# Heads' value products, x's forms, pool gates and tail stores moved to other slots of a hand-ordered transformer block

## The chip, the cores and the metric

The kernel runs on one core of a Trainium2 chip. The metric is the device time of one execution in microseconds (us); the median of several executions is compared. Five engines work side by side, each through its own instructions in order: TensorE (PE, matrix products and 128x128 transposes; PEld is its loading of the stationary operand), VectorE (DVE), ScalarE (ACT), GpSimd (POOL) and SyncE (SP, which here only issues transfers). Products end up in PSUM, which the kernel uses as eight banks of 128 x 512 fp32.

## The reference

One layer of a block on x (256 tokens x 4096) with a memory of 256 tokens:

```
h = rmsnorm(x, g_mix_pre);  proj = h @ w_in            # 4096 -> q|k|v|gate_a (4 x 2048), u|gate_b (2 x 2048)
A: 16 heads of 128: chunk-causal attention over the own chunk of 64 and earlier ones, bias by relative distance
   y_a = attention * silu(gate_a)
B: 4 groups of 512: trailing mean of u over 2/4/8/16 tokens, minus u; a 512x512 map; a scale
   y_b = pooled * silu(gate_b)
x = x + rmsnorm(concat(y_a, y_b) @ w_out, g_mix_post)
m = rmsnorm(mem, g_mem);  q = rmsnorm(x, g_xa_pre) @ w_xq;  k, v = m @ w_xk, m @ w_xv
x = x + rmsnorm(cross_attention(q, k, v, 4 heads) @ w_xo, g_xa_post)
```

All data is fp32.

## The kernel before

**Precision.** An fp32 operand a is used as a = h + l, both in a rounded fp32 format: ACT copies (rounds) a to h, DVE computes l = a - h, and a product of two such operands takes three matmuls (h h, l h, h l: lines 308 to 310). Each weight piece of 128 x 1024 thus costs one ACT cast (L185, `wh`) and one DVE difference (L186, `wl`).

**Slots.** The weights are a stream of 648 pieces of 512 KB. `plan` writes the stream; piece i is multiplied in slot i (`mm`), 12 matmuls of 512 columns as a rule. The last loop of `block_kernel` goes through the slots and in each one issues, in this order: `firsts` (set by `first_at`), `jobs` (the casts and differences of a piece that PE needs two or three slots later, and the load of a later one), `tasks` (set by `at`), and then the slot's own matmuls. So a function's place in the lists is its place in every engine's instruction order. Five pieces of `wh` and `wl` fit into SBUF, four raw pieces.

**Pairs.** w_in and w_out are taken in pairs of strips, 32 slots a pair: A0, B0, A1, B1, A2, B2, A3, B3 (gate_a and v, then q and k, of four heads each), U0 to U3 (u and gate_b of a pool group), O0 to O3 (w_out). A pair goes over 16 chunks of two 128-row blocks of its input (two slots each). A0, B0 and O0 are direct: four products per slot. The others do chunks 4, 6, 8, 10, 12 and 14 with seven products instead of eight (a Strassen step: `quad_sums`, `quad_split`, `quad_rest` make sums of weights on DVE; 12 matmuls in the first slot, 9 in the second). A pair's products are collected in banks: four at its start, a fifth at slot 8, a sixth and a seventh at slot 9, until `early` (slot 30) and `late1`, `late2` at its end read them. Every other product takes a bank from a list, first in first out (`bank`), and gives it back when its reader is issued (`done`); whoever takes it next waits for that reader.

**Forms of x.** A0 uses x as loaded. For the pairs after it, `x_forms(c)` makes chunk c's normalised blocks: two scaled blocks (L535), then one difference (L543) or the four sums of `sums_of` (L385 to L388), then h and l of all of them (`split_copy`, L237 on ACT and L238 on DVE). The 16 chunks stand in slots 19 to 41, two in three slots, while A0 and B0 run; `load_x` is issued three slots ahead.

**Heads.** With e the end of a B pair, head j of its group has o = e + 6 + 7j: `head_scores` in slot o, `head_max` (L615, reads the scores' bank) first in o+1, `head_exp` o+2, `head_soft` o+3, `head_turn` (three transposes) o+5, `head_turned` first in o+6, `head_att` (value product, L600 and L651) in o+8, `head_y` (multiply with the gate, L659) o+9, `y_store` (to a scratch in DRAM) o+11. `a_keep` turns the two gate results into `sg` (two `turn`s: four transposes each into a bank, then an ACT copy, L488) and makes v's h and l.

**Pool.** After pair U g: `pool_u` turns u, `pool_sum` and `pool_d` make the means for two halves b on DVE (with an h on ACT and an l on DVE), `pool_gates` runs `gate` twice (tanh on ACT, L494, then DVE, L495; one buffer for the tanh), `pool_turn` turns the gates into `sg`, two slots of pool products follow at slots 8 and 9 of the next pair, and `pool_y` collects a result and multiplies (L319, L320, L731).

**Memory norm and tail.** `rm.all_at` puts the sums over squares of the memory (`Rms.sums`, L269), their root and its use into successive slots. The last eight output blocks are made tokens-first, half t of the tokens after the other: `tail_stat` squares a result from its bank with its sum (L1069), `tail_root` and `tail_spread` make the norm, `tail_copy` copies the bank (L1086), `tail_turn` transposes it, `tail_gain`, `tail_scale` (L1104) and `tail_out` (L1110, add and store) finish. A store is issued by the ACT queue if POOL added, and by SP if DVE did.

Of the kernel before, what the change touches and what calls it, by code (L numbers as in the profile page):

```python
# [12 lines left out]
AF = mybir.ActivationFunctionType  # L13
# [32 lines left out]
QUADS = KT // 2  # L46
# [63 lines left out]
def block_kernel(ctx: ExitStack, tc: tile.TileContext, x, mem, ws, relb, vecs, out):  # L110
    nc = tc.nc
# [25 lines left out]
    def buf(tag, shape, name, dtype=F32, bufs=1):  # L137
        return com.tile(shape, dtype, tag=tag, name=name, bufs=bufs)
# [3 lines left out]
    def at(i, f, *a):  # L142
        tasks.setdefault(i, []).append((f, a))

    def first_at(i, f, *a):

        firsts.setdefault(i, []).append((f, a))
# [4 lines left out]
    def tiles(ap):  # L152
        return ap.rearrange("p (a b) -> p a b", b=P)

    def tok(t):
        return slice(t * P, t * P + P)

    V, A, T_ = nc.vector, nc.scalar, nc.tensor
# [3 lines left out]
    ev = {k: buf(f"e_{k}", [P, 512], f"e_{k}") for k in ("t", "u2", "u3", "c")}  # L162
# [56 lines left out]
    for s in range(n):  # L219
# [6 lines left out]
        else:  # L226
            i = s - (2 if wide and m[1] > FAST[0] else 3)
# [7 lines left out]
    def split_copy(h, l, src):  # L235

        A.copy(h, src)  # L237
        V.tensor_sub(l, src, h.bitcast(F32))  # L238
# [84 lines left out]
    accs = {}  # L323
# [14 lines left out]
    def end(*key):  # L338
        return max(where[key].values())
# [4 lines left out]
    for tag, cs in (("Fb1", (0, 1, 2, 3)), ("Fb2", (5, 7)), ("Fa1", (4, 6, 8, 9, 11)), ("Fa2", (10, 12, 13, 14, 15))):  # L344
        o = 0
# [3 lines left out]
    for tag, cs in (("Fb1", (0, 1, 2, 3, 5, 7)), ("Fa1", (4, 6, 8, 9, 11)), ("Fa2", (10, 12, 13, 14, 15))):  # L349
        o = 0  # L350
# [13 lines left out]
    def block(stage, c):  # L364

        tag, o, u = HOME[stage, c]
        f = forms[tag][:, 256 * o:256 * (o + u)]
        return tiles(f[:, :u * P]), tiles(f[:, u * P:])
# [14 lines left out]
    def sums_of(a11, a21, a12, a22, dst):  # L383

        V.tensor_add(dst[:, 1, :], a21, a22)  # L385
        V.tensor_sub(dst[:, 2, :], dst[:, 1, :], a11)
        V.tensor_sub(dst[:, 3, :], a11, a21)
        V.tensor_sub(dst[:, 0, :], a12, dst[:, 2, :])  # L388
# [50 lines left out]
    def result(pair):  # L439

        names = ("t", "u3", "u2", "c") if pair[0] == "O" else ("t", "c", "u2", "u3")
        return dict(zip(("c11", "c21", "c12", "c22"), (ev[k] for k in names)))
# [48 lines left out]
    def gate(pair, k):  # L491

        g, th = result(pair)[k], hd["x7"][:, 512:]
        A.activation(th, g, AF.Tanh, scale=0.5)  # L494
        V.scalar_tensor_tensor(g, th, 1.0, g, op0=OP.add, op1=OP.mult)  # L495

    for pair in PAIRS:
        if pair not in DIRECT:
            at(slot[pair, FAST[-1], 1] + 1, early, pair)
        e = end_slot[pair]  # L500
# [5 lines left out]
    hd = {"x7": buf("X7", [P, 1024], "x7"), "x6": buf("X6", [P, 1024], "x6")}  # L506
# [20 lines left out]
    def x_forms(c):  # L527
        src = xch.pop((1, c))
        ft = tiles(hd["ft"][c % 2])
        R = tiles(rx.R)  # L530
        spots = ((6, 8), (0, 2)) if c in FAST else ((0, 2), (3, 5))
        for j in range(2):
            k = 2 * c + j
            a, b = spots[j]
            V.scalar_tensor_tensor(ft[:, a:b, :], tiles(src[:, j, :]), gv[:, G_MIX_PRE + k:G_MIX_PRE + k + 1], R,  # L535
                                   op0=OP.mult, op1=OP.mult)
        h, l = block("in", c)
        u = h.shape[1]
        if c in FAST:
            sums_of(ft[:, 6, :], ft[:, 7, :], ft[:, 0, :], ft[:, 1, :], ft[:, 2:6, :])  # L540
        else:
            q = ft[:, :6, :].rearrange("p (k f) b -> p k f b", f=3)
            V.tensor_sub(q[:, :, 2, :], q[:, :, 0, :], q[:, :, 1, :])  # L543
        split_copy(h, l, ft[:, :u, :])
        if c in FAST:
            j = FAST.index(c)
            e = hd["extra"][j // 4][:, 256 * (j % 4):256 * (j % 4) + 256]
            extra[c] = e[:, :P], e[:, P:]
            split_copy(*extra[c], ft[:, 7, :])
# [5 lines left out]
    first = KT // 2 + 3  # L555
    at(first - 3, x_buffers)
    for c in range(QUADS):
        i = first + (3 * c) // 2
        at(i - 3, load_x, c, 1)
        at(i, x_forms, c)  # L560


    def a_gates(hg):
# [101 lines left out]
    for hg in range(4):  # L665
        e = end_slot["A", hg]
        at(e + (3 if hg else 14), a_gates, hg)
        at(e + (9 if hg else 16), a_keep, hg)
        e = end_slot["B", hg]
        at(e + 2, b_turn, hg, 0)  # L670
        at(e + 3, b_turn, hg, 1)
        for j in range(4):
            h, o = 4 * hg + j, e + 6 + 7 * j
            at(o - 3, head_bias, h)
            at(o - 2, head_qk_split, h)
            at(o, head_scores, h)
            first_at(o + 1, head_max, h)
            at(o + 2, head_exp, h)
            at(o + 3, head_soft, h)
            at(o + 5, head_turn, h)  # L680
            first_at(o + 6, head_turned, h)
            at(o + 8, head_att, h)
            at(o + 9, head_y, h)
            at(o + 11, y_store, h, "sg", j)


    pg = {}
# [27 lines left out]
        hl = pg["d"][b]  # L715
        split_copy(hl[:, :, :S], hl[:, :, S:], d)

    def pool_gates(g):
        gate(("U", g), "c12")
        gate(("U", g), "c22")  # L720

    def pool_turn(g):
        for t, k in enumerate(("c12", "c22")):
            turn(("U", g), k, hd["sg"][:, :, tok(t)], 0.5)
# [8 lines left out]
    for g in range(4):  # L733
        e = end_slot["U", g]
        at(e + 2, pool_u, g)
        i = [e + 3, e + 4]
        for b in range(2):
            for j in range(g + 1):
                at(i[b], pool_sum, g, b, j)
            at(i[b] + 1, pool_d, g, b)  # L740
        at(e + 5, pool_gates, g)
        at(e + 7, pool_turn, g)
        for c in range(4):
            j = end("pool", g, c)
            at(j + 1 + c % 2, pool_y, g, c)
            at(j + 3 + c % 2, y_store, 16 + 4 * g + c, "sg", c)


# [18 lines left out]
    for c in range(QUADS):  # L767
        i = slot[("O", 0), c, 0] - 3
# [7 lines left out]
    def x2(k, m=1):  # L776
        return x2t[k // 4][:, k % 4:k % 4 + m, :]
# [12 lines left out]
    for m in range(4):  # L790
        e = end_slot["O", m]
# [29 lines left out]
    rm = Rms("m", None, None, None, None)  # L821
# [18 lines left out]
    def m_pass(slots, home, stat=False):  # L840

        for kt, i, j in slots:
            if kt % 2 == 0:
                at(j, load_m, kt // 2, home)
            at(i, m_prep, kt, stat)
            if stat and kt % 2:
                at(i + 1, rm.add)

    uses = sorted(where["xk",].items())
    at(uses[0][1] - 8, late_buffers)  # L850
    m_pass([(k, i - 3, i - 6) for k, i in uses], 0, True)
    rm.all_at(uses[-1][1] - 1)
    m_pass([(k, i - 2, i - 6) for k, i in sorted(where["xv", 1].items())], 1)

    kv = {}
# [56 lines left out]
    b = e_out + 10  # L912
    room = begin("xq", 0) - b - 1
    for c in range(KT // 2):
        i = b + (c * room) // (KT // 2)
# [79 lines left out]
    e = end("xq", 7)  # L995
    for h in range(XH):
        i = end("xq", 2 * h + 1)
# [4 lines left out]
    for h in (0, 1):  # L1002
        i = end("xq", 2 * h + 1)
# [8 lines left out]
    e = end("xv", 1)  # L1012
# [23 lines left out]
    for c in range(first_tail):  # L1036
        e = end("xo", c) + 1
# [20 lines left out]
    zs = const.tile([P, 2, 2], F32, name="zs")  # L1058
# [6 lines left out]
        done(rz.p)  # L1065

    def tail_stat(t, j):
        a = accs["xo", j, t]
        A.activation(ev["u2"], a, AF.Square, accum_out=zs[:, t, j:j + 1])  # L1069
        b = z["b"] = z["base"][:, t:t + 1] if j == 0 else z["b"]  # L1070
        v = const.tile([P, 1], F32, name=f"v_z{t}{j}")
        V.tensor_scalar(v, zs[:, t, j:j + 1], 1.0 / D, b, op0=OP.mult, op1=OP.add)
        z["b"] = v
# [34 lines left out]
    def tail_out(t, eng, a, b):  # L1108
        y = y2["y"][:, a:b, tok(t)]
        eng.tensor_add(y, y, x2(a, b - a)[:, :, tok(t)])  # L1110
        (nc.scalar if eng is nc.gpsimd else nc.sync).dma_start(out[:, a:b, tok(t)], y)

    v, g = nc.vector, nc.gpsimd
    s_, o_ = tail_scale, tail_out
    at(n - TAIL + 3, tail_base)
    for t in range(2):
        e = n - TAIL // 2 + TAIL * t
        at(e, tail_stat, t, 0)
        at(e, tail_copy, t, 0)
        at(e + 1, tail_turn, t, 0)  # L1120
        at(e + 2, tail_gain, t, 0)
    e = n
    at(e, tail_stat, 0, 1)
    at(e, tail_root, 0)
    at(e, tail_copy, 0, 1)
    at(e + 2, tail_turn, 0, 1)
    at(e + 2, tail_spread, 0)
    at(e + 3, tail_gain, 0, 1)
# [1 line left out]
    for i, steps in enumerate((((s_, 0, 4), (o_, g, 0, 4), (s_, 4, 12), (o_, v, 4, 8)),  # L1130
# [3 lines left out]
        for f, *a in steps:  # L1134
            at(e + 3 + i, f, 0, *a)
    e = n + TAIL
    at(e, tail_stat, 1, 1)
    at(e, tail_root, 1)
    at(e, tail_copy, 1, 1)
    at(e, tail_turn, 1, 1)  # L1140
    at(e, tail_spread, 1)
    for f, *a in ((s_, 0, 4), (o_, v, 0, 4), (s_, 4, 12), (o_, g, 4, 8), (s_, 12, 16), (o_, g, 8, 12), (s_, 16, 24),
# [156 lines left out]
```

## Time and profile before

| | |
|---|---|
| median of 3 runs | 1888.58 us (1888.17 to 1889.97) |
| profiled execution | 1889.54 us, span 1887.8 us |
| PE, DVE, ACT busy | 97%, 79%, 55% of the span |
| mean granted TensorE clock | 0.987 of full speed |

The span runs from the first to the last instruction. Idle time stands in brackets, with what ended it. A matmul's duration overlaps the next one's, so PE's rate is read from start to start.

### The profile page before, as it was taken

To read this page: it belongs to the slowest core of one execution; us is meant where nothing else is said; L and a number is where in the kernel's file an instruction comes from. 1 tells how busy PE (TensorE), PEld (TensorE's weight loads), DVE (VectorE), ACT (ScalarE), POOL (GpSimd) and SP (SyncE) were. 2 spreads that over 40 slices of the span, in tenths; PEclk is the share of its full clock that TensorE was granted. 3 is DMA by queue.
4 is the path that set the end of the run, shared out by engine and by line. 5 is a ranking of instruction groups with operands and counts; after the bars stand their busy time and mean duration, and the time that the engine had idled before them with its cause. 6 is when DMAs were issued, how large, how long until landed. Compare 5 with 4: busy or idle time off the path is not lost.

```text
span 1887.8 us, 23776 instructions
## 1 busy us (share of the span) xinstructions
PE 1823.7 (97%) x8404; PEld 1508.0 (80%) x8404; DVE 1498.0 (79%) x1999; ACT 1033.6 (55%) x1411; POOL 17.3 (1%) x20
## 2 busy tenths in 40 slices
PE   9989999999999999999999999999999999999996
PEld 7867878877887788777888787888888888888885
DVE  8875687978797889787989898769788899656686
ACT  8455454645554555454545465555555677545552
POOL 0000000000000000000000000000000000000002
PEclk9999999999999999999999999999999999999998
DMA  8756555655565556454656476756565777556654
GB/s 291 235 189 214 168 184 178 212 189 178 184 221 167 181 195 219 168 178 156 217 173 226 168 242 206 257 170 213 186 215 182 240 259 256 189 173 215 208 186 121
DMA packets 122920, 378.14 MB, mean 200 GB/s; under 512 B 12976, under 2 KB 27440, under 8 KB 122800
## 3 DMA queue, kind: packets, MB, share of 16 engines
q1 hardware_dynamic: 118432, 374.25, 59.5%
q10 hardware_dynamic: 4368, 2.36, 0.4%
q8 instruction: 66, 1.08, 0.2%
q14 instruction: 54, 0.44, 0.1%
HBM read 368.17 MB, written 8.39 MB: 199 GB/s over the span
## 4 chain that ended last, share of the span: by engine, by line
PE 85%; DVE 8%; issue 3%; ACT 2%; DMA 1%; POOL 0%; SPq 0%; ACTq 0%; DVEq 0%; POOLq 0%
PE P L308 17%; PE P L309 17%; PE P L310 17%; PE acc L303 6%; DVE wl L186 3%; PE acc L304 3%; PE c L310 3%; PE c L308 3%; PE c L309 3%; ACT wh L185 1%; PE xk L308 1%; PE xv L309 1%; PE xk L309 1%; PE xv L310 1%; PE xv L308 1%
## 5 line engine op out<-in xcount | busy, mean ns | idle before, releaser
L186 DVE TENSOR_TENSOR wl<-raw,wh 128x1024 fp32r<-128x1024 f32 (+1 forms) x646 | 782.4, 1221 | 244.1 <-ACT wh L185 232.1
L185 ACT CAST wh<-raw 128x1024 fp32r<-128x1024 f32 (+1 forms) x646 | 672.0, 1049 | 349.0 <-PE P L309 78.9
L308 PE MATMUL P<-wh,Fa 128*128 128x512 f32 x938 | 370.9, 395 | 4.0 <-DVE x L320 3.8
L309 PE MATMUL P<-wh,Fa 128*128 128x512 f32 x938 | 367.8, 392 | 0.0
L310 PE MATMUL P<-wl,Fa 128*128 128x512 f32 x938 | 367.7, 392 | 0.0
L308 PE MATMUL P<-wh,Fb 128*128 128x512 f32 x588 | 234.2, 398 | 0.0
L310 PE MATMUL P<-wl,Fb 128*128 128x512 f32 x588 | 230.3, 392 | 0.0
L309 PE MATMUL P<-wh,Fb 128*128 128x512 f32 x588 | 230.3, 392 | 0.0
L185 ACT CAST wh<-tt 128x1024 fp32r<-128x1024 f32 (+1 forms) x156 | 123.8, 834 | 168.6 <-DVE tt L209 147.8
L308 PEld LDWEIGHTS P<-wh,Fa 128*128 128x128 f32 x938 | 178.2, 190 | 42.5 <-issue 4.9
L310 PEld LDWEIGHTS P<-wl,Fa 128*128 128x128 f32 x938 | 177.6, 189 | 37.6
L309 PEld LDWEIGHTS P<-wh,Fa 128*128 128x128 f32 x938 | 178.2, 190 | 35.8
L186 DVE TENSOR_TENSOR wl<-tt,wh 128x1024 fp32r<-128x1024 f32 (+1 forms) x156 | 143.4, 956 | 43.4 <-ACT wh L185 42.4
L310 PEld LDWEIGHTS P<-wl,Fb 128*128 128x128 f32 x588 | 111.2, 189 | 23.8
L309 PEld LDWEIGHTS P<-wh,Fb 128*128 128x128 f32 x588 | 111.6, 190 | 22.0
L308 PEld LDWEIGHTS P<-wh,Fb 128*128 128x128 f32 x588 | 111.5, 190 | 21.9
L310 PE MATMUL c<-wl,Fa 128*128 128x512 f32 x276 | 108.5, 393 | 3.1 <-DVE wl L186 3.1
L308 PE MATMUL c<-wh,Fa 128*128 128x512 f32 x276 | 108.5, 393 | 1.2 <-ACT wh L185 1.2
L309 PE MATMUL c<-wh,Fa 128*128 128x512 f32 x276 | 107.5, 390 | 0.0
L303 PE MATMUL acc<-h2HL,wh 128*128 128x512 f32 x256 | 91.4, 400 | 0.0
L304 PE MATMUL acc<-h2HL,wl 128*128 128x256 f32 x256 | 71.8, 281 | 0.0
L303 PE MATMUL acc<-xoHL,wh 128*128 128x512 f32 x192 | 66.9, 395 | 0.0
(291 smaller groups left out, 2405.0 us busy)
## 6 DMA issues: line engine op xcount, KB each, us to landing
raw<-ws_dram SPq DMA_DIRECT2D x647, 512.0 KB, 3.9
tt<-x_dram SPq DMA_DIRECT2D x31, 256.0 KB, 4.9
lc<-mem_dram SPq DMA_DIRECT2D x24, 256.0 KB, 4.4
yd<-sg SPq DMA_DIRECT2D x32, 128.0 KB, 4.6
yin<-yd SPq DMA_DIRECT2D x16, 256.0 KB, 5.0
lc<-x_dram SPq DMA_DIRECT2D x16, 256.0 KB, 4.3
x<-relb_dram SPq DMA_DIRECT2D x16, 192.0 KB, 4.5
e_u<-mem_dram SPq DMA_DIRECT2D x8, 256.0 KB, 4.1
```

The source lines that it names most:

```text
L185: A.copy(h[:, c], src[:, c])
L186: V.tensor_sub(l[:, c], src[:, c], h[:, c].bitcast(F32))
L303: T_.matmul(acc, H[:, w], X, start=first, stop=last, skip_group_check=True)
L304: T_.matmul(acc[:, :S], L[:, w], X[:, :S], start=False, stop=last, skip_group_check=True)
L308: T_.matmul(acc, xs[0], w[0], start=first, stop=False)
L309: T_.matmul(acc, xs[1], w[0], start=False, stop=False)
L310: T_.matmul(acc, xs[0], w[1], start=False, stop=last)
```

## The change

Five edits of order, none of arithmetic. (1) `x_forms` keeps the scaled blocks and sums and moves to the head of its slot (`first_at`); h and l move into `x_split`, at the head of the slot after. (2) `head_att`, `head_y` and `y_store` come one slot later, and `a_keep` of groups 1 to 3 too (slot 10 instead of 9). (3) The pool's two gates stand apart (slots e+4 and e+6 instead of both in e+5), group 0's sums and means come one slot later, `pool_turn` too (e+8); all four `pool_y` move to the head of the slot behind their product. (4) The memory's sums come one slot later. (5) In the tail the bank is copied before the square, which reads the copy; the stores of POOL's blocks of the first token half go out on SP's queue.

```
-        split_copy(h, l, ft[:, :u, :])
+    def x_split(c):
+        ft = tiles(hd["ft"][c % 2])
+        h, l = block("in", c)
+        split_copy(h, l, ft[:, :h.shape[1], :])
         if c in FAST:
...
-        at(i, x_forms, c)
+        first_at(i, x_forms, c)
+    for c in range(QUADS):
+        first_at(first + (3 * c) // 2 + 1, x_split, c)
...
-        at(e + (9 if hg else 16), a_keep, hg)
+        at(e + (10 if hg else 16), a_keep, hg)
...
-            at(o + 8, head_att, h)
-            at(o + 9, head_y, h)
-            at(o + 11, y_store, h, "sg", j)
+            at(o + 9, head_att, h)
+            at(o + 10, head_y, h)
+            at(o + 12, y_store, h, "sg", j)
...
         at(e + 2, pool_u, g)
-        i = [e + 3, e + 4]
         for b in range(2):
+            i = e + 3 + b + (g == 0)
             for j in range(g + 1):
-                at(i[b], pool_sum, g, b, j)
-            at(i[b] + 1, pool_d, g, b)
-        at(e + 5, pool_gates, g)
-        at(e + 7, pool_turn, g)
+                at(i, pool_sum, g, b, j)
+            at(i + 1, pool_d, g, b)
+            at(e + 4 + 2 * b, gate, ("U", g), ("c12", "c22")[b])
+        at(e + 8, pool_turn, g)
         for c in range(4):
             j = end("pool", g, c)
-            at(j + 1 + c % 2, pool_y, g, c)
+            first_at(j + 1, pool_y, g, c)
...
-    rm.all_at(uses[-1][1] - 1)
+    rm.all_at(uses[-1][1])
...
-        a = accs["xo", j, t]
-        A.activation(ev["u2"], a, AF.Square, accum_out=zs[:, t, j:j + 1])
+        A.activation(ev["u2"], ev["tc"[j]], AF.Square, accum_out=zs[:, t, j:j + 1])
...
-        (nc.scalar if eng is nc.gpsimd else nc.sync).dma_start(out[:, a:b, tok(t)], y)
+        (nc.scalar if t and eng is nc.gpsimd else nc.sync).dma_start(out[:, a:b, tok(t)], y)
...
-        at(e, tail_stat, t, 0)
         at(e, tail_copy, t, 0)
+        at(e + 1, tail_stat, t, 0)
...
+    at(e, tail_copy, 0, 1)
     at(e, tail_stat, 0, 1)
     at(e, tail_root, 0)
-    at(e, tail_copy, 0, 1)
...
+    at(e, tail_copy, 1, 1)
     at(e, tail_stat, 1, 1)
     at(e, tail_root, 1)
-    at(e, tail_copy, 1, 1)
```

## Rows read from the trace of the kernel before

**Rows 1.** The page, part 1: busy us (share of the span) xinstructions.

```profile
PE 1823.7 (97%) x8404; PEld 1508.0 (80%) x8404; DVE 1498.0 (79%) x1999; ACT 1033.6 (55%) x1411; POOL 17.3 (1%) x20
```

**Rows 2.** Timeline of PE, second head group: start, us, line, operation [idle before].

```profile
465.12 0.39 PE L308 MATMUL P<-wh,Fa 128*128 128x512 f32 x1
465.80 0.39 PE L308 MATMUL P<-wh,Fa 128*128 128x512 f32 x1
...
469.41 0.58 PE L600 MATMUL at<-ahl,vs 128*128 128x256 f32 x1 [2.77 <-DVE x L615]
```

**Rows 3.** Windows: us, busy of PE, PEld, DVE, ACT, POOL; PEclk; DMA share; GB/s.

```profile
80.00:90.00 10.00, 10.00 (x46) 8.29 (x45) 7.99 (x15) 4.09 (x6) 0.00 (x0) 1.00 0.59 185
101.00:147.00 46.00, 38.17 (x150) 26.61 (x150) 37.08 (x63) 23.63 (x32) 0.00 (x0) 1.00 0.53 175
284.50:292.00 7.50, 7.43 (x28) 6.21 (x29) 4.49 (x8) 3.44 (x7) 0.00 (x0) 0.77 0.42 134
838.50:846.50 8.00, 7.90 (x25) 6.52 (x26) 3.82 (x7) 2.73 (x5) 0.00 (x0) 0.61 0.40 125
```

**Rows 4.** Waits of PE: engine line waited for: us in total, times, longest.

```profile
PE at L600 <- DVE x L615: 23.3, 12, 2.8
PE tn L484 <- DVE e_u L495: 6.5, 5, 3.2
PE P L308 <- DVE x L320: 3.8, 2, 3.4
...
PE ms L269 <- DVE lc L261: 1.8, 1, 1.8
...
PE tn L1092 <- ACT e_t L1086: 0.6, 1, 0.6
```

**Rows 5.** Timeline of DVE, one cycle of x's forms in pair B0.

```profile
97.97 0.88 DVE L535 SCALAR_TENSOR_TENSOR ft<-tt,gv,x 128x256 f32<-128x256 f32 x2
...
100.21 0.96 DVE L238 TENSOR_TENSOR Fb<-ft,Fb 128x768 fp32r<-128x768 f32 x1 [0.90 <-ACT Fb L237]
101.16 2.36 DVE L186 TENSOR_TENSOR wl<-raw,wh 128x1024 fp32r<-128x1024 f32 x2
...
106.38 1.09 DVE L238 TENSOR_TENSOR Fa<-ft,Fa 128x896 fp32r<-128x896 f32 x1 [1.01 <-ACT Fa L237]
...
107.59 1.22 DVE L186 TENSOR_TENSOR wl<-raw,wh 128x1024 fp32r<-128x1024 f32 x1
108.72 0.88 DVE L535 SCALAR_TENSOR_TENSOR ft<-tt,gv,x 128x256 f32<-128x256 f32 x2
```

**Rows 6.** The page, part 6: the loads of x; last, us to landing.

```profile
tt<-x_dram SPq DMA_DIRECT2D x31, 256.0 KB, 4.9
```

**Rows 7.** Timeline of DVE in the second head group.

```profile
433.31 1.23 DVE L186 TENSOR_TENSOR wl<-raw,wh 128x1024 fp32r<-128x1024 f32 x1 [1.82 <-ACT wh L185]
...
468.81 0.55 DVE L615 SCALAR_TENSOR_TENSOR x<-sc,x 128x384 f32<-128x384 f32 x1
```

**Rows 8.** Timelines of PE and ACT at a_keep of the second group.

```profile
322.57 1.03 PE L484 MATMUL tn<-ident,e_u 128*128 128x128 f32 x8
...
325.20 2.00 ACT L185 CAST wh<-raw 128x1024 fp32r<-128x1024 f32 x2
```

**Rows 9.** Timelines of ACT, SP (group 0) and DVE (group 3), pool gates.

```profile
879.10 1.08 ACT L488 ACTIVATE sg<-tn 128x512 f32<-128x512 f32 x2 [5.63 <-DMA yd<-sg]
...
875.14 0.42 SPq L663 DMA_DIRECT2D yd<-sg  x1
...
1159.01 0.69 DVE L495 SCALAR_TENSOR_TENSOR e_u<-x,e_u 128x512 f32<-128x512 f32 x1 [0.70 <-ACT x L494]
```

**Rows 10.** Timelines of ACT, PE and DVE in the tail.

```profile
1870.80 0.60 ACT L1069 ACTIVATE e_u<-xo 128x512 f32<-128x512 f32 x1 [6.22 <-POOL y L1110]
...
1872.02 1.04 PE L1092 MATMUL tn<-ident,e_c 128*128 128x128 f32 x4 [2.62 <-ACT e_c L1086]
...
1873.58 0.69 DVE L1104 TENSOR_TENSOR y<-y,mr 128x512 f32<-128x512 f32 x1 [0.89 <-PE mr L1082]
```

More of the change, by code (lines that the diff above doesn't have):

```diff
@@ L536, in x_forms @@
                                    op0=OP.mult, op1=OP.mult)
-        h, l = block("in", c)
-        u = h.shape[1]
         if c in FAST:
@@ L716, in pool_d @@
         split_copy(hl[:, :, :S], hl[:, :, S:], d)
-    def pool_gates(g):
-        gate(("U", g), "c12")
-        gate(("U", g), "c22")
     def pool_turn(g):
```

## The prediction, made before the change was run

> **What bounds the kernel now.** I read the page's busy shares first [rows 1]: TensorE (PE) is at work 97% of the span, so the change can only win what PE loses: gaps, and stretches at the lower clock. At the full clock three of its 512-column matmuls start in 0.68 us, from 465.12 to 465.80 [rows 2], so 0.227 us each, and a slot of twelve takes 2.72 us. The windows [rows 3] show a full stretch (80 to 90), a stretch that loses (101 to 147) and two in which the granted clock is far below 1.00: after a long wait PE runs for some us at the lower of its levels, 1.2 GHz instead of 2.4. The share missing times the length is what that costs: 0.23 x 7.5 = 1.7 us in the first, which stands for six like it among the heads, 0.39 x 8.0 = 3.1 us in the second. PE's own waits [rows 4] then name the places: twelve waits of the heads' value products (L600), five before the pool's gate transposes, two for banks that the pool results free, one before the memory sums, one in the tail. The rest, but for the first loads and what follows the last product, is PE at full rate, which no part of the diff shortens.
>
> **x's forms.** In 101 to 147 PE starts 150 matmuls: 150 x 0.227 = 34.0 of 46.0 us [rows 3], so 12.0 us are lost. The reason stands in VectorE's (DVE's) timeline [rows 5]: from one form to the same place three slots later, 97.97 to 108.72, it needs 10.75 us where PE needs 3 x 2.72 = 8.16. Of the 10.75 it waits 0.90 + 1.01 for ScalarE's (ACT's) rounded copy of the form that it has just made. After the change the copy is asked for in the next slot: DVE has that slot's weight difference (half of 2.36, so 1.18) to do while ACT copies for about 0.9 to 1.0, and ACT's weight cast no longer stands behind a copy that waits for DVE. DVE is left with 8.84 us per three slots, 0.68 more than PE. Six such triples (chunks 4 to 15) put it 4.1 us behind. It has that much in hand: 80 to 90 is full although DVE was already at 10.75 per 8.16, so from 80 to 101 alone it used up 21 x (1 - 8.16/10.75) = 5.1 us of lead. So nearly all comes back: I take 11.5, bounds 0 (the tie stays, or x comes too late) and 12.0. The load of x keeps its slot while the form moves up by one weight difference; two slots, 5.4 us, remain against 4.9 from issue to landing [rows 6]. It is the closest margin in this part.
>
> **Heads.** The value product waits for L615, whose result it doesn't read. Seven of the eight PSUM banks belong to the running pair from its ninth slot on; the scores of the next head take the last one, L615 frees it, and the value product takes it. So it waits until DVE has come to L615. One slot later PE has another 2.72 us of matmuls to run first. But DVE limits what that gives: in the second group it works with few waits, and PE's third wait ends when DVE gets to L615 at 468.81, behind the weights of the pair [rows 2, 7]. An earlier PE meets the same DVE at the scores, at the transposes or at a weight. So I don't add up twelve waits; I ask when the third of a group ends. There the slot's matmuls fit into the 2.77 us of wait [rows 2]: 2.7 x 4 groups = 10.9. The slow clock behind it goes with it if the rest is short: 1.7 x 3 + 3.1 = 8.2. And in groups 2 to 4 the first wait costs a slow stretch as well, in which PE frees weight buffers late and DVE stands idle 1.82 us (before 433.31 [rows 7]; three such): 5.4. Sum 24.5. Low end: 10.9 without the rest. High end: all twelve waits, 23.3 [rows 4], and seven slow stretches, 6 x 1.7 + 3.1: 36.6. I stay near the middle, because of DVE. The head's multiply now comes behind the next slot's weights and the next transposes two slots behind it instead of three. Behind those transposes stand PE's matmuls, but DVE is the later of the two there, so I add nothing.
>
> **a_keep at slot 10.** This costs. Its two turns (eight transposes) now run back to back, at 322.57 [rows 8], because three banks are free at slot 9. At slot 10 the pair has opened its seventh, one is left, and the second turn must wait until ACT has copied the first. PE comes to slot 10 about 2.0 us later (nine matmuls), at 324.6, and is through the first turn at 325.1. ACT's copy stands behind the slot's two weight casts, which end at 327.2 now [rows 8] and earlier when the results aren't copied ahead of them. Bounds of PE's wait: 0.6 (only the copy) and 2.7 plus a slow stretch of 1.7. I take 1.5; three groups (the first keeps its slot): 4.5 lost, bounds 1.8 and 13.2. Behind the waiting turn stand the slot's matmuls.
>
> **Pool.** In the first group ACT waits 5.63 us for the last head's store before it may overwrite the gate buffer [rows 9]; the store is issued only at 875.14, since SyncE (SP) first waits to issue a raw load, behind DVE's differences and both gates. PE loses 3.8 us to it [rows 4] and a slow stretch of about 1.7. With the second pool form and one gate moved behind the weight difference (the gate alone is 0.69 and a wait of 0.70), SP gets to the store sooner, and ACT reaches the overwriting copy a slot later, with two casts ahead of it. I take 5.3 (0 to 5.5). In the other groups PE waits 6.5 us for the gates in five waits [rows 4], the longest, 3.2, in the last group, with a slow stretch of about 1.7 behind it. The first gate now comes a slot earlier, the second loses DVE's 0.70 us of waiting for ACT's tanh [rows 9], and the turns are asked for 2.72 us later. In the last group about 1.9 stay (second form, a weight, a gate), so 3.3 come back; in the two between, where DVE is full right behind, 1.3 and 1.5. Sum 6.1 (2 to 8.2). The results' earlier copies open the pair's banks sooner but make ACT wait for the pool matmuls ahead of two casts: nothing either way, at most 1 per group.
>
> **Memory sums and tail.** One slot (2.72) covers the 1.8 us wait for the last sum [rows 4]: 1.8 (0.5 to 1.9). In the tail ACT begins its last square at 1870.80, after 6.22 us behind a store that waits for POOL; PE's last product was done 2.62 us before its transposes at 1872.02, so at 1869.40 [rows 10]. With these stores on SP, ACT copies at 1869.4 and squares about 0.55 later: 0.85 earlier, and the 0.6 that PE waited for the first copy goes too [rows 4]. The end follows from there by DVE alone, from 1873.58. With rounding I take 1.6 (0 to 2.2). SP's stores are not what ends.
>
> The Trainium skill, "DMA: Bandwidth & Descriptors", section "Issuing engines are not separate DMA queues", says that initiating DMAs on several engines saves only the sequencer's time to initiate. By that rule the tail edit would give nothing on the path, and the sum would be 1.6 smaller. The trace differs here through ACT's wait in front of the issue [rows 10], so I keep the row.
>
> **Sum.** 11.5 + 24.5 - 4.5 + 5.3 + 6.1 + 1.8 + 1.6 = 46.3. The profiled execution took 1889.54 us (span 1887.8 and 1.7 around it): 1843.2. The median of the three runs is 0.96 lower, so 1842.3; I say 1842.
>
> **Rivals.**
> *DVE is the bound in heads and pools.* The waits move to scores, turns and weights and stay long enough to drop the clock. For: DVE's cycle and the third wait. Against: it had idle time in each group. Then heads give 10.9, a_keep costs 9, pools 5, with 11.5 and 3: 21.4, so 1867.
> *DVE gives way*, since much of its waiting is on a late PE: forms 12.0, heads 36.6, a_keep -1.8, pools 13.7, the rest 4.1: 64.6, so 1824. Against: its timeline before the third wait shows hardly any waiting on PE.
> The Trainium skill, "Perfetto Trace Analysis", "Identifying the Most-Contended Engine", measures TensorE by its weight loads instead of its matmuls; 1508.0 us of them [rows 1] at 8.29 per 10 of a full stretch [rows 3] make an estimated 1819 us of floor, and this rival stays above it.
> *The forms' step does nothing*: x lands late, or ACT's copy still comes last. Then 11.5 less: 1854.
> *Slower: the one spare bank.* Eight head turns and three a_keep turns depend on who frees it. If DVE's multiply is so late that each of the eleven waits over 4.6 us more than I count (46.3 + 4.5 for a_keep, over 11), the gain is gone; at 6 us each the time is about 1904. Against: DVE's multiply is two slots, 4.8 us or more, ahead of its reader.
>
> **How the numbers follow.** Forecast 0.62 (its own range 1830 to 1855), DVE bound 0.16, forms idle 0.10, DVE gives way 0.08, slower or cancelled 0.04. A difference under 0.2%, 3.8 us, is what a measurement of this kernel can't tell from none. Range 1826 to 1865: it holds the forecast's own range and the idle forms, and leaves out the upper half of the first rival's spread, the lower half of "DVE gives way", and the last, with the forecast's tails about 2 in 10. Faster 0.96, same 0.01, slower 0.03.
>
> **What would show it.** Right: 101 to 147 as full as 80 to 90, and DVE's forms without a wait for ACT; at L600 four waits under 2 us at most, the clock near 1.00 behind them; three waits of 1 to 2 us at a_keep's second turn; no DMA wait of ACT before the gate buffer; the last square about 1.6 us sooner against the end. Wrong: a long wait at a form (x late), at the scores or the head turns with a low clock behind it, or weights that come late through whole pairs.

## The result and the profile after

The changed kernel took 1847.18 us (median of 4 runs, 1847.08 to 1847.51) against 1888.87 for the kernel before in the same session: a ratio of 0.9779, 95% interval 0.9762 to 0.9796, so 41.7 us less. The forecast was 1842.0, range 1826 to 1865. The profiled run took 1847.51 us, its span 1845.6.

Part 1 of the page of the changed kernel answers to [rows 1]:

```profile
PE 1804.0 (98%) x8404; PEld 1497.9 (81%) x8404; DVE 1494.1 (81%) x1999; ACT 1032.5 (56%) x1411; POOL 17.3 (1%) x20
```

The counts of PE, DVE, ACT and POOL are those of before: no work was taken away. What went is waiting, and time at the lower clock: PE's busy time fell by 19.7 us, and the mean granted clock of the profiled runs rose from 0.987 to 0.997 (share missing times span, an estimate: 24.5 us before, 5.5 after). The waits of PE in the changed kernel answer to [rows 4] (its lines stand 4 further down from the forms on, 1 less in the tail: L604 was L600, L619 was L615, L648 was L644):

```profile
PE sc L610 <- ACT x L648: 6.0, 4, 1.5
PE tn L484 <- ACT sg L488: 4.2, 3, 1.4
PE pt L642 <- DVE x L636: 4.0, 8, 0.7
PE at L604 <- DVE x L619: 3.7, 4, 0.9
PE tn L484 <- DVE e_u L495: 2.5, 1, 2.5
PE mr L1081 <- DVE tt L1077: 1.3, 1, 1.3
PE acc L303 <- ACT sg L488: 1.3, 1, 1.3
...
```

The value product's 23.3 us in twelve waits have become 3.7 in four. The scores (L610) and the head turns (L642), which had no such wait, now wait 10.0 us together, and a_keep's second turn (L484 for ACT's L488) 4.2 in three. The five gate waits have become one. The windows over x's forms and over the middle head groups (columns as in [rows 3]):

```profile
101.00:147.00 46.00, 46.00 (x209) 38.16 (x208) 37.91 (x57) 26.36 (x34) 0.00 (x0) 1.00 0.65 226
...
350.00:850.00 500.00, 485.91 (x2238) 399.72 (x2237) 416.95 (x558) 269.94 (x371) 0.00 (x0) 1.00 0.57 193
```

101 to 147 is full, and the clock in 350 to 850 is 1.00: with the new waits, 1.5 us at most, it stayed up.

To see where the time came from, I compare the starts of ACT's copies of the turned results, instructions that no edit moved: the first of the first and of the fourth head group (q), of each pool group (u), of the output's first pair (x2). In us from the span's start, for the kernel before, three of its variants (below) and the changed kernel; the last line is the span:

```
mark        before  forms_alone  heads_alone  pools_alone   changed
q, first    204.76       193.08       204.08       204.96    190.89
q, fourth   757.32       747.25       748.81       759.12    735.22
u, 1        858.82       847.59       844.01       860.59    831.54
u, 2        955.61       943.70       939.31       951.53    922.48
u, 3       1047.61      1035.67      1031.29      1041.86   1012.81
u, 4       1141.13      1129.23      1126.44      1133.56   1104.65
x2, first  1241.13      1230.37      1226.40      1231.95   1203.39
span        1887.8       1878.4       1873.0       1880.0    1845.6
```

The profiled spans differ by 42.1 us (unrounded): 13.9 up to the first q, 13.4 from there to u 1, 5.9 in the first pool group, 1.7, 1.7 and 1.3 in the other three stretches, 4.4 behind them (2.0 around the memory sums, 2.2 in the tail, 0.2 between). Of the 13.9 the forms are 11.7 (forms_alone). The other 2.2 are within what programs that are alike up to that mark scatter (190.9 to 193.1 over eight runs), so the forms' share is known to about 2 us.

The stretch from the first q to u 1, the heads' own, in the kernel before and in the changed one (columns as in [rows 3]):

```profile
204.76:858.82 654.06, 630.80 (x2855) 520.55 (x2854) 534.28 (x708) 348.31 (x478) 0.00 (x0) 0.98 0.56 188
190.89:831.54 640.65, 621.72 (x2855) 511.03 (x2854) 532.52 (x707) 347.18 (x477) 0.00 (x0) 1.00 0.57 191
```

PE's idle time falls by only 4.3 us, from 23.3 to 18.9. Its busy time falls by 9.1 for the same number of instructions, at a granted clock of 1.00 instead of 0.98: about two thirds of the heads' gain come with the clock.

### The profile page after: what moved, and what is told of

Same layout as the page of the kernel before. It is cut to its first block, busy times and chain, and to the rows that moved or that the text cites. A ratio compares the mean times of both kernels' runs of the same rounds, so it can differ in the third digit from the quotient of the medians.

```text
span 1845.6 us, 23768 instructions
## 1 busy us (share of the span) xinstructions
PE 1804.0 (98%) x8404; PEld 1497.9 (81%) x8404; DVE 1494.1 (81%) x1999; ACT 1032.5 (56%) x1411; POOL 17.3 (1%) x20
## 5 line engine op out<-in xcount | busy, mean ns | idle before, releaser
L308 PEld LDWEIGHTS P<-wh,Fa 128*128 128x128 f32 x938 | 176.2, 188 | 35.6
L309 PEld LDWEIGHTS P<-wh,Fa 128*128 128x128 f32 x938 | 176.2, 188 | 35.4
```

Source lines behind the costliest of these rows:

```text
L308: T_.matmul(acc, xs[0], w[0], start=first, stop=False)
L309: T_.matmul(acc, xs[1], w[0], start=False, stop=False)
```

## Experiments

Each set had runs of the kernel before on its own chip (medians 1891.52, 1891.53 and 1892.83 us), so times are compared by ratio: against 0.9779 for the changed kernel.

### The parts alone, on the kernel before

forms_alone takes from the diff `x_split`, `first_at(i, x_forms, c)` and its loop; pools_alone takes the pool's loop; heads_alone takes these lines:

```diff
-        at(e + (9 if hg else 16), a_keep, hg)
+        at(e + (10 if hg else 16), a_keep, hg)
-            at(o + 8, head_att, h)
-            at(o + 9, head_y, h)
-            at(o + 11, y_store, h, "sg", j)
+            at(o + 9, head_att, h)
+            at(o + 10, head_y, h)
+            at(o + 12, y_store, h, "sg", j)
```

> The kernel before with the two steps of x's forms alone. By the prediction's term: 11.5 us less, 1877 us, the stretch 100 to 150 full, and no wait of DVE for ACT in its forms; the rest of the trace as before. Rival, the parts are not independent (a form stretch without gaps only moves a wait into the first pairs): less than 6 us less, above 1882 us, with new PE waits behind 150 us.

> The kernel before with the value products, their multiplies and stores one slot later, and a_keep at slot 10. By the prediction's terms 24.5 less and 4.5 more: 20 us less, 1868.5 us; by what the changed kernel's trace shows at these places (about 22.5 back, 4.8 lost) 1871. Waits of PE at the value products four, under 1 us each, three waits of 1.4 us at a_keep's second turn. Rival, DVE bound: the gain is below 12 us, over 1876 us, with a clock below 1.00 in the head groups.

> The kernel before with the pool's forms, gates, turns and results at the new slots alone. By the prediction's terms 5.3 and 6.1 less: 11.4 us less, 1877.2 us; by what the changed kernel's trace shows at these places (5.8, 1.3, 2.5 and 0.9) 10.5 less, 1878 us. In the first group ACT no longer waits for the last head's store before it overwrites the gate buffer. Rival, the gain at the first group came from the heads' later slots and not from this: about 5 us less, 1884 us, and the wait for the store is still there.

Measured: forms 1877.41 us, ratio 0.9921 (0.9902 to 0.9939); heads 1876.26, 0.9916 (0.9902 to 0.9931); pools 1881.68, 0.9946 (0.9930 to 0.9963). Each part is a gain by itself. The marks size them more closely than the times do (forms_alone's four runs lie between 1872.5 and 1880.2 us, and its profile is of the longest): the forms 11.7 up to the first q; the heads 15.6 from the first q to u 2; the pools 10.95 from u 1 to x2 (5.85, 1.67, 1.82, 1.61). They don't quite add up: in the first pool group the heads' edit alone gives 1.5 and the pools' alone 5.85, and both together 5.85. And from the first q to u 1 forms_alone and pools_alone, which change nothing there, need 654.5 and 655.6 us against 654.1, so differences under about 2 us say little. The heads are the part that came out short, 15.6 where the prediction had 20.0. In heads_alone ACT still waits 5.1 us for the last head's store before it overwrites the gate buffer; in pools_alone that wait is gone, so that gain was the pools' own.

### Which resource the value product waited for

```diff
-        t, p, d = hd["x7"][:, 384:512], hd.pop(("pt", h)), hd["hl"]
+        t, p, d = hd["pb"][:, :], hd.pop(("pt", h)), hd["hl"]
```

(`pb` is a new buffer; the value product's last matmul reads it.)

> The kernel before, with the third block of the transposed softmax in a buffer of its own, so that nothing which the value product reads shares a buffer with what DVE's L615 writes. Theory, the value product waits for the PSUM bank that L615 frees: the twelve waits stay, 23 us in all, time within 0.2% of 1888.6 us. Rival, it waits for the shared buffer x7: the waits at the value product go, and at least 10 us of the time with them.

Measured: 1892.03 us in one run, and the value product still waits 23.3 us in twelve for L615, longest 2.8. The shared buffer was not the cause; what is left in common between the two is the bank, as the prediction read from the kernel's list of banks. No run gave the value product another bank.

### Where the heads' missing gain went

Four edits of the changed kernel, one at a time. akeep_slot9 puts `a_keep` back at `e + 9`. copy_first changes the order of three instructions in `head_turned`:

```diff
-        split_copy(d[:, 1, :S], d[:, 1, S:], p[:, :S])
+        A.copy(d[:, 1, :S], p[:, :S])
         A.copy(t, p[:, S:384])
+        V.tensor_sub(d[:, 1, S:], p[:, :S], d[:, 1, :S].bitcast(F32))
```

softmax_on_act changes `head_soft`:

```diff
-            V.tensor_scalar(e[:, c], e[:, c], st[:, 6 + t:7 + t], None, op0=OP.mult)
+            A.activation(e[:, c], e[:, c], AF.Copy, scale=st[:, 6 + t:7 + t])
```

> The changed kernel with a_keep of groups 2 to 4 back at slot 9. Theory, at slot 10 the pair leaves one spare bank and the second turn waits for the first one's copy: with three banks free the three waits (4.2 us in the rows) go and the time falls by 4 to 5 us, to 1843. Rival, ACT must then wait for the last head's store, which is now issued one slot later, before it overwrites the gate buffer: a DMA wait at ACT's copy of the turn, and less than 1.5 us gained.

> The changed kernel with ACT's copy of the third transposed block put ahead of DVE's difference of the first two. Theory, the scores' wait (four, 6.0 us in all) hangs on ACT's last copy, which itself stands behind DVE's difference: the bank comes free about 0.4 us sooner each time, ACT's casts behind it too, 1.5 to 3 us less, 1845. Rival, DVE alone sets the pace among the heads: the wait stays, with DVE's difference named instead of ACT's copy, within 1 us of 1847.2.

> The changed kernel with the two multiplications that normalize the softmax moved from DVE to ACT (16 heads, about 0.63 us each, 10 us of DVE's work). Theory, DVE is what bounds the head groups: the waits at the scores, the transposes and the value products (13.7 us in all) shrink by about 6, time near 1841. Rival, the order on ACT sets it: the multiplications stand behind weight casts, the transposes wait longer, 1850 or more.

Measured: akeep_slot9 1842.63 us, ratio 0.9745 (0.9728 to 0.9761); copy_first 1833.10, 0.9694 (0.9680 to 0.9708); softmax_on_act 1869.25, 0.9883 (0.9868 to 0.9898). From the first q to u 1 they need 635.0, 625.3 and 660.8 us, the changed kernel 640.7.

So slot 10 for a_keep costs 5.6 us, and its three waits are gone at slot 9, where three banks are free: that fits the spare bank, and ACT's copy doesn't come to wait for the store.

copy_first won 14.4 us between the profiled spans, 15.3 from the first q to u 1, where I expected 1.5 to 3, and softmax_on_act took 8 us of work from DVE (1494.1 to 1486.4) and lost 20. copy_first leaves DVE's work as it was (1493.2 us busy), so it tells against my theory that this work bounds the heads; softmax_on_act alone would not, since it gives ACT something new to wait for (below). ACT's and DVE's timelines in the changed kernel, at the last head of the second group:

```profile
461.48 0.37 ACT L237 CAST ahl<-pt 128x256 fp32r<-128x256 f32 x1
464.38 0.27 ACT L648 COPY x<-pt 128x128 f32<-128x128 f32 x1 [2.52 <-DVE ahl L238]
464.54 2.00 ACT L185 CAST wh<-raw 128x1024 fp32r<-128x1024 f32 x2
...
462.73 0.68 DVE L462 TENSOR_TENSOR e_t<-e_t,P 128x512 f32<-128x512 f32 x1
463.33 0.68 DVE L463 TENSOR_TENSOR e_c<-e_u,P 128x512 f32<-128x512 f32 x1
463.93 0.42 DVE L238 TENSOR_TENSOR ahl<-pt,ahl 128x256 fp32r<-128x256 f32 x1
465.62 1.23 DVE L186 TENSOR_TENSOR wl<-raw,wh 128x1024 fp32r<-128x1024 f32 x1 [1.28 <-ACT wh L185]
```

ACT stands idle 2.52 us in front of its copy of the third block (L648) until DVE's difference (L238) of the other two is done, though the copy reads nothing that L238 writes. Behind it in ACT's queue stand weight casts. So as soon as DVE has released ACT, DVE itself must wait 1.28 us for the cast that its next weight difference needs. Each engine waits for the other in turn, one idle while the other works: that is why DVE looked like the bound. It stood so in the kernel before already, here at the group's third head:

```profile
461.66 0.27 ACT L644 COPY x<-pt 128x128 f32<-128x128 f32 x1 [2.73 <-DVE ahl L238]
462.91 2.36 DVE L186 TENSOR_TENSOR wl<-raw,wh 128x1024 fp32r<-128x1024 f32 x2 [1.28 <-ACT wh L185]
```

The last head of the second group in copy_first:

```profile
456.08 0.37 ACT L647 CAST ahl<-pt 128x256 fp32r<-128x256 f32 x1 [0.86 <-PE pt L642]
456.35 0.27 ACT L648 COPY x<-pt 128x128 f32<-128x128 f32 x1
456.50 1.06 ACT L185 CAST wh<-raw 128x1024 fp32r<-128x1024 f32 x1
...
457.07 0.68 DVE L463 TENSOR_TENSOR e_c<-e_u,P 128x512 f32<-128x512 f32 x1
457.67 0.42 DVE L649 TENSOR_TENSOR ahl<-pt,ahl 128x256 fp32r<-128x256 f32 x1
458.00 1.22 DVE L186 TENSOR_TENSOR wl<-raw,wh 128x1024 fp32r<-128x1024 f32 x1
```

No idle time in front of the copy, none in front of the difference. Over the whole run, the waits of ACT and DVE in the changed kernel,

```profile
ACT x L648 <- DVE ahl L238: 41.2, 16, 3.6
...
DVE wl L186 <- ACT wh L185: 249.6, 279, 3.1
```

and in copy_first, where the wait of L648 is no longer among them:

```profile
DVE wl L186 <- ACT wh L185: 234.4, 263, 3.1
```

DVE's waits for casts fall by 15.2 us, the time up to the last mark by 14.4. PE's waits at the scores, the head turns and the value products fall from 13.7 us to 3.8, all at the scores, now for DVE's difference. In softmax_on_act another wait of that kind is added, sixteen times: ACT's multiplication stands in front of the casts until DVE's reciprocal is there. The instructions of that line:

```profile
L636 ACT ACTIVATE x<-x,st x32: 401/448/496, 216.1 to 844.4; 128x128 f32<-128x128 f32 x16, 128x256 f32<-128x256 f32 x16
...
  DVE st L634: 39.7, 16
```

ACT stands still for 39.7 us there, and PE comes to u 1 20.1 us later. What was expected there as the rival (behind the casts, the transposes wait) isn't what happened either: the transposes' waits went from 4.0 to 3.6 us and the scores' from 6.0 to 15.1.

Then the change's own step for the heads may treat a symptom. The kernel before with the new order of copy_first and nothing else:

> The kernel before, value products still eight slots behind, with ACT's copy of the third transposed block ahead of DVE's difference, and nothing else. Theory, ACT standing in its queue behind that difference (16 waits, 33.9 us in the kernel before), with weight casts behind it, is what makes DVE late at L615: without it the twelve waits at the value products shrink by half or more and the time falls by 10 to 20 us, to about 1875. Rival, the value product needs its later slot whatever ACT does, since L615 stands in the same slot as its reader: the waits stay above 18 us and the time within 4 us of before.

Measured: 1862.31 us, ratio 0.9840 (0.9823 to 0.9856), 30.5 us less, where the heads' part of the change gave 0.9916. The value products' waits, without any later slot:

```profile
PE at L600 <- DVE x L615: 8.4, 8, 1.1
```

From the first q to u 1 it needs 625.9 us. copy_first, with the later slots and a_keep at 10, needs 625.3; combined (below), with the later slots and a_keep at 9, 620.1. So behind the right order the slot move is worth 5.8 us, and a_keep's slot 10 takes 5.2 of them back. Why L648 waited stays partly open. The wait stands in the program: in the trace all sixteen copies carry a wait for the semaphore that DVE's instructions raise, and in copy_first none does. The buffer that the copy writes isn't the reason, for in own_tile_att, where it has one of its own, the wait is still there:

```profile
ACT pb L646 <- DVE ahl L238: 34.0, 16, 2.8
```

What is left in common is the PSUM bank that both lines read. A bank of its own for the third block wasn't tried.

### The second step of x's forms

```diff
-        first_at(first + (3 * c) // 2 + 1, x_split, c)
+        at(first + (3 * c) // 2, x_split, c)
```

> The changed kernel with x's forms still at the head of their slot, but their copy and differences at the end of the same slot instead of the next one. The prediction's step, what counts is that ACT's copy is asked for with a slot of DVE's other work in between: about 11 us of the loss in 100 to 150 come back, 1858 us, DVE waits for the copy of its forms. Rival, it is enough that the form stands ahead of the slot's weight difference and the copy behind the slot's cast: the stretch stays full, within 2 us of 1847.2.

Measured: 1847.32 us, ratio 0.9763 (0.9748 to 0.9777); 101 to 147 is full, 46.00 of 46.00. The rival holds. DVE's timeline of this kernel:

```profile
98.78 0.87 DVE L535 SCALAR_TENSOR_TENSOR ft<-tt,gv,x 128x256 f32<-128x256 f32 x2
99.69 0.43 DVE L541 TENSOR_TENSOR ft<-ft 128x256 f32<-128x256 f32 x1
100.03 1.22 DVE L186 TENSOR_TENSOR wl<-raw,wh 128x1024 fp32r<-128x1024 f32 x1
101.17 0.95 DVE L238 TENSOR_TENSOR Fa<-ft,Fa 128x768 fp32r<-128x768 f32 x1
```

The form stands ahead of the slot's weight difference and the rest behind it; ACT copies in between. No wait is left at L238 in this stretch (it was 0.90 and 1.01, [rows 5]). From one wide difference to the next, 97.58 to 106.16, DVE needs 8.58 us; in the changed kernel 97.45 to 106.02, 8.57. The prediction said 8.84 for it. The move to the next slot adds nothing.

### The last pool group

```diff
-            at(e + 4 + 2 * b, gate, ("U", g), ("c12", "c22")[b])
+            at(e + (4 if g == 3 else 4 + 2 * b), gate, ("U", g), ("c12", "c22")[b])
```

> The changed kernel with the last pool group's second gate at the slot of its first. Theory, that gate is late because it stands behind the second form and a weight difference on DVE: the wait of 2.5 us at the turn goes and that of 1.3 behind it shrinks, 2.5 to 3.5 us less, 1844. Rival, the second form becomes late by the gate's 0.7 us and the products wait instead: within 1 us of 1847.2.

Measured: 1848.51 us, ratio 0.9775 (0.9760 to 0.9789): no gain. The wait of 2.5 us for the gate is gone, but the one behind it grew, from 1.3 to 3.7:

```profile
PE acc L303 <- ACT sg L488: 3.7, 1, 3.7
```

From the fourth u to x2 it needs 99.9 us, the changed kernel 98.7. ACT's timeline shows why, and it is the heads' mechanism once more:

```profile
1123.19 0.61 ACT L237 CAST Fa<-yin 128x512 fp32r<-128x512 f32 x1
1126.29 0.62 ACT L237 CAST Fa<-tt 128x512 fp32r<-128x512 f32 x1 [2.49 <-DVE tt L388]
1126.81 1.04 ACT L185 CAST wh<-raw 128x1024 fp32r<-128x1024 f32 x1
1127.76 1.08 ACT L488 ACTIVATE sg<-tn 128x512 f32<-128x512 f32 x2
```

The copy that frees the gates' banks (L488) stands behind a cast of the output's forms, which waits 2.49 us for DVE's sums. The gate was late, but it was not what PE waited for last.

### The tail's stores

```diff
-        (nc.scalar if t and eng is nc.gpsimd else nc.sync).dma_start(out[:, a:b, tok(t)], y)
+        (nc.scalar if eng is nc.gpsimd else nc.sync).dma_start(out[:, a:b, tok(t)], y)
```

> The changed kernel with the first half's GpSimd stores issued by ACT again; the copies stay ahead of the squares. By the row (ACT waits 6.22 us in front of its last square for stores that wait for POOL): the last copy and square come 0.5 to 1 us later against PE's last product, the end by 0.5 to 1. By the rule that the issuing engine doesn't matter: the last square stands where it is, the end too. The time can't tell these apart, the profile's tail can.

Measured: 1852.04 us, ratio 0.9788 (0.9773 to 0.9802), which doesn't tell it from 0.9779. ACT's timeline does, first in the changed kernel,

```profile
1822.72 0.59 ACT L1085 COPY e_t<-xo 128x512 f32<-128x512 f32 x1 [4.79 <-PE xo L310]
...
1828.65 0.58 ACT L1085 COPY e_c<-xo 128x512 f32<-128x512 f32 x1 [4.59 <-PE xo L310]
1829.27 0.63 ACT L1068 ACTIVATE e_u<-e_c 128x512 f32<-128x512 f32 x1
```

and with the stores on ACT:

```profile
1824.36 2.24 ACTq L1110 DMA_DIRECT2D out_dram<-y  x2
1826.65 0.63 ACT L1068 ACTIVATE e_u<-e_t 128x512 f32<-128x512 f32 x1 [2.96 <-POOL y L1109]
...
1831.75 0.59 ACT L1085 COPY e_c<-xo 128x512 f32<-128x512 f32 x1 [4.38 <-POOL y L1109]
1832.37 0.63 ACT L1068 ACTIVATE e_u<-e_c 128x512 f32<-128x512 f32 x1
```

In the changed kernel each copy is released by PE's last product of its block; with the stores on ACT the last copy is released by POOL, and PE's last turn waits 3.9 us for it instead of 0.7:

```profile
PE tn L1091 <- ACT e_c L1085: 3.9, 1, 3.9
```

DVE's last addition starts at 1844.58 instead of 1841.18, although the tail began 0.27 sooner: 3.7 us, against the 0.5 to 1 that I expected. The Trainium skill, "DMA: Bandwidth & Descriptors", section "Issuing engines are not separate DMA queues", says that initiating DMAs on several engines saves only the sequencer's time to initiate. By that nothing would have changed here. For the transfers themselves no run speaks against it; what these rows show is that the issuing instruction stands in ACT's queue until POOL has written what it stores.

tail_act is also the tail's other half by itself, the copy ahead of the square with the stores where they were. From the first product into the tail's banks (`xo`) to DVE's last addition the kernel before needs 39.0 us, the changed kernel 37.2 and tail_act 40.8: without the stores' move the copies lose 1.8 us, and only both together win. The stores' move without the copies was not tried.

### Together

copy_first, akeep_slot9 and gate_early, and the turns of the last pool group at `e + 7`, so that ACT copies them ahead of the output's forms.

> The changed kernel with ACT's copy of the third block first, a_keep back at slot 9, and in the last pool group the second gate at the slot of the first and the turns one slot earlier (ahead of the y forms on ACT). From the single runs: 14.4 for the copy, 5.7 for a_keep, and 2.5 to 3.5 for the pool if the turn's copy now comes ahead of the forms: 22 to 24 less, 1824 us. Rival, once ACT is no longer blocked a_keep's wait is hidden anyway or the pool's wait only moves again: 1827 to 1833.

Measured: 1824.75 us, ratio 0.9642 (0.9628 to 0.9657), faster than both kernels and 68 us below the kernel before. Its longest waits of PE:

```profile
PE sc L610 <- DVE ahl L649: 3.7, 4, 0.9
PE c L310 <- DVE wl L186: 1.5, 4, 0.5
PE mr L1082 <- DVE tt L1078: 1.3, 1, 1.3
PE warm L1205 <- DVE half L1201: 1.1, 1, 1.1
```

From the fourth u to x2 it needs 95.2 us (1085.66 to 1180.89), the changed kernel 98.7: the 3.5 us that the early gate alone didn't give.

## Why the prediction was right, and where it was off

The sum was 46.3 us; 41.7 came (42.1 between the profiled spans). The sign held in every part, the mechanism in all but the heads and the last pool group, where it held in part. Some of the closeness is luck: the heads with a_keep came out 6.6 us short in the changed kernel (13.4 against 20.0), and 2.2 us within the scatter of the first loads made up a third of that.

- **x's forms:** 11.5 predicted, 11.7 measured, good to about 2 us. The reason given (a weight difference between DVE's form and its second use) held; the second slot for it was not needed, as split_same_slot shows.
- **Heads:** this is the step that was off. 24.5 predicted; 13.4 net up to u 1 and a_keep's 5.6 make 19.0. (heads_alone has 14.1 net there, and 1.5 more in the first pool group that the pools' edit gives anyway.) All waits at the value product were to go but for four under 2 us: it came so, four of 0.9 at most, and the clock stayed up. What failed is the size of the terms. The waits were to give 10.9 of their 23.3: 19.6 went, 10.0 came new at the scores and the head turns (for the turns the sum had nothing, "so I add nothing"), and PE's idle time without a_keep's 4.2 fell by 8.5. The slow clock, and DVE's standing idle with it, were to give 8.2 and 5.4 on top; PE's busy time fell by 9.1. I had the new waits in view as DVE's limit. The limit was there, but not for the reason given: DVE came late because ACT's casts came late, and these because ACT stood behind L238. It could be read ahead: in the kernel before, ACT had stood idle for 2.73 us in front of its copy at 461.66, and DVE for 1.28 us in front of its weight difference at 462.91, on the way to L615 at 468.81 [rows 7]. "It works with few waits" was a wrong reading: between 401 and 469.4 DVE waits 10.8 us for casts, in ten waits. I took DVE's idle 1.82 before 433.31 for the mark of a late PE, and never read ACT's queue there.
- **a_keep:** 4.5 predicted, 5.6 by akeep_slot9, 4.2 of it in the three waits.
- **Pools:** 11.4 predicted, 10.95 alone, 10.5 in the changed kernel. The first group 5.3 against 5.85; the two between 1.3 and 1.5 against 1.7 and 1.8; the last 3.3 against 1.6 alone and 1.3 in the changed kernel. I had read the gate as what PE waits for last. Behind it stood ACT's copy of the turns, in the queue behind the output's forms.
- **Memory sums and tail:** 1.8 and 1.6 predicted, 2.0 and 2.2 measured, the first with a scatter: forms_alone and pools_alone lose 1.6 at the same place by no edit of theirs. The stores were weighed rightly, by the row; with the copies first they hold more than was counted, 3.7 us. That the copies lose without the stores' move wasn't seen ahead.
- **Rivals:** "DVE is the bound" was right that the waits move to scores and turns, and wrong in the rest: the clock didn't fall, and 8 us less of DVE's work made the kernel slower. "The one spare bank" cost 5.6 us and stayed far from deciding. The forms' step did its work. The floor of 1819 us, which the prediction estimates with a measure of the Trainium skill ("Perfetto Trace Analysis", "Identifying the Most-Contended Engine"), is not passed by any kernel here: the best took 1824.75. It is a rough floor: the same sum with the changed kernel's rows (1497.9 us, 38.16 per 46.00) gives an estimated 1806.

## What to carry to other kernels

When an engine looks like the bound because its idle times are short, look at what releases each of them, and at what that releaser itself stood behind: two engines that wait for each other in turn are both late, though neither is busy all the time. An instruction that waits holds all that follows in its engine's queue, so ask of each wait what stands behind it; here one copy, put ahead of an instruction of another engine that it doesn't read, gave twice the gain of moving the readers a slot later (28.2 us against 14.1, from the first q to u 1 on the kernel before). Before a late result is made earlier, check that nothing else is due right behind it, or the wait only changes its name.

## What was not expected of the hardware

ACT's copy of the third block waited sixteen times, 41.2 us in all, up to 3.6 us each, for a DVE instruction whose output it doesn't read; with the order turned there were no such waits. It is the program that sets this wait, by a semaphore, and not the chip that was seen to make one. Both instructions read one PSUM bank; whether that is the program's reason stays open. The multiplication by a per-row factor took ACT 0.40 to 0.50 us for 128 and 256 columns, and DVE 0.29 to 0.35; moving it cost 20 us all the same, by what it waited for and not by its length.
